# One core, one inference step of a hybrid encoder: four transfers put in other places

## The chip, the core and the metric

The kernel runs on one core of a Trainium2 chip. A core has a matrix engine (PE, TensorE), a vector engine (DVE), a scalar engine (ACT), a general engine (POOL, GpSimd) and a queue engine (SP), which run their own instruction lists in order and wait for one another through semaphores. Transfers are issued from the lists of SP, ACT and POOL and run on the core's 16 DMA engines. The metric is device time in microseconds (us) of the whole program, the median of several runs.

## The reference

```python
h = rmsnorm(x, norm_g)
q, k, v, za, fl, bg, cg, hc, zc = split(h @ w_in)       # columns of one 1024 x 4104 weight
logf = log_sigmoid(fl + b_f);  u = cg * hc
o_a = fox_attention(q, k, v, cumsum(logf))              # 8 heads x 64, causal, with a forget bias
y_c = bg * causal_conv(u, conv_w)                       # depthwise, width 3: conv_w is (3, 512)
x = x + concat(o_a * silu(za), y_c * silu(zc)) @ w_out
y = rmsnorm(x, final_g)
```

This is done for one prompt of 16 meta tokens and 2048 tokens, and for a sample of 8 streams of 16 tokens, each with 256 cached rows. Keys, values, log-forget values and the last convolution inputs are outputs too. All is float32.

## The kernel before

**The work.** Each product of the reference is made of three matmuls: both operands are split into a high and a low part (`hh`, `hl` for tokens, `wh`, `wl` for weights), and high x high, low x high and high x low are summed in a PSUM tile `ps`, of which there are two.

**The stages.** Positions go in two groups. Group 0 has 1280 positions of the prompt and the sample's 128 tokens, group 1 the rest. For each group: `normalise` loads token tiles of 128 rows (`xt`, four buffers), squares them on ACT (`sq`), scales them on DVE and transposes them on PE through `sp`; `values` (first half, `q` = 0) multiplies each of group 0's 11 token tiles with half of the value weights (`wvh`, `wvl`), 24 matmuls a tile; then come keys, queries and gates in slices of 128 columns (`project`), attention units, and the convolution. Projections, attention and the convolution of a group are interleaved on PE. At the end `output` multiplies 17 tiles (the sample's first, then the prompt's 16) with the output weight and normalises the rows.

**What sets the order.** A planner (`Times`) keeps a modelled time for every instruction and every transfer: generators yield a ready time, and `weave` steps the one that is ready soonest. PE's list is the order in which this happens. The lists of DVE, ACT, POOL and SP are sorted by modelled time in `settle`. So a transfer that is moved or that gets cheaper in the model changes the modelled times of what comes after, and with them the order on every engine.

**The parts that the change touches.**
- `load_constants` (L381) loads the mask and, in three transfers (L387), the convolution taps `cw` (channels on partitions: 512 separate 4-byte elements each), and halves them on DVE (L389).
- `split_wv` (L508) splits half of the value weights into `wvh` and `wvl`, and at once stores both to `wv_d` (L535, L536; 1088 and 1024 KB) for group 1, which loads them back. Stores are issued by POOL (`STORES`, L1591).
- `values` (L653): after each tile's matmuls ACT copies `ps` to `sv` (two buffers), which frees `ps`; POOL stores `sv` to the output and the split values `vv` to `v_d`.
- `split_w` (L479) loads the next weight slice `raw` (issued by ACT, L500 to L502), which ACT casts to `wh`; the planner lists this cast on ACT among the copies of `ps` and `sv`.
- `output` (L1364): `load(n)` calls `output_load` (L1337), which loads a tile's concatenated activations `cr` from `cat_d`, casts them to `ch` (ACT) and subtracts to `cl` (POOL). The first tile's are loaded long before (L1353). In `run`, `load_out` (L1577, L1582) loads the rest of the output weight's pieces `o`, three kinds of old weight buffers (`raw`, `wh`, `wl`) serving as room for the first of them, then `fg`, the final norm's weights (L1583), and only then does `output` begin (L1390) and load the second tile's `cr`.

Of the kernel before, what the change touches and what calls it, by code (L numbers as in the profile page):

```python
# [11 lines left out]
F32 = mybir.dt.float32  # L12
F32R = mybir.dt.float32r
BF16 = mybir.dt.bfloat16
AF = mybir.ActivationFunctionType
ALU = mybir.AluOpType
# [4 lines left out]
P = 128  # L21
D = 1024
NC = 8
# [19 lines left out]
OFF_Q, OFF_K, OFF_V, OFF_ZA, OFF_FL = 0, 512, 1024, 1536, 2048  # L43
# [220 lines left out]
def stream(g):  # L264
    return [g, None, False]
# [49 lines left out]
class Step:  # L315
# [7 lines left out]
    def dma(self, out, in_, by=None):  # L323

        if out.dtype == F32R:
            out = out.bitcast(F32)
        if in_.dtype == F32R:
            in_ = in_.bitcast(F32)
        return getattr(self.nc, by or (STORES if out.space == DRAM else "sync")).dma_start(out=out, in_=in_)
# [51 lines left out]
    def load_constants(self, pool):  # L381
        nc, dma = self.nc, self.dma
        mraw = pool.tile([P, P], F32, name="mraw")
        dma(out=mraw, in_=self.cst[:, C_MASK:C_MASK + P])
        nc.vector.tensor_copy(out=self.mask, in_=mraw)
        for i in range(3):
            dma(out=self.cw[:, :, i], in_=self.conv_w[0, i].rearrange("(c p) -> p c", p=P))  # L387

        nc.vector.tensor_scalar(out=self.cw, in0=self.cw, scalar1=0.5, scalar2=None, op0=ALU.mult)  # L389


    def spans(self, ph, c0, n):
# [115 lines left out]
    def split_wv(self, q, raws, pool=None, then=None):  # L508


        nc = self.nc
        wh = self.vp.tile([P, NC, 272], F32R, name="wvh")
        wl = self.vp.tile([P, NC, 256], F32R, name="wvl")
        if OFF_V + 256 * q in self.w_d:
            dh, dl = self.w_d[OFF_V + 256 * q]
            n = 272 if q == 0 else 256
            for k in range(2):
                sl = slice(4 * k, 4 * k + 4)
                self.dma(out=wh[:, sl, :n], in_=dh[:, sl, :n])
                self.dma(out=wl[:, sl], in_=dl[:, sl])  # L520
            return wh, wl
        if q == 0:
            raw8 = pool.tile([P, NC, H], F32, name="raw8")
            self.dma(out=raw8, in_=self.w_v[:, :, OFF_FL:OFF_FL + H])
        for k in range(2):
            raw, sl = raws(k), slice(k * P, k * P + P)
            nc.scalar.copy(out=wh[:, :, sl], in_=raw)
            getattr(nc, V_E).tensor_tensor(out=wl[:, :, sl], in0=raw, in1=wh[:, :, sl].bitcast(F32), op=ALU.subtract)
            if then:
                then()  # L530
        if q == 0:
            nc.vector.tensor_copy(out=wh[:, :, 256:264], in_=raw8)
            nc.vector.tensor_tensor(out=wh[:, :, 264:272], in0=raw8, in1=wh[:, :, 256:264].bitcast(F32), op=ALU.subtract)
        self.w_d[OFF_V + 256 * q] = dh, dl = [self.dram.tile([P, NC, n], F32R, name=f"wv_d{q}{n}") for n in (272, 256)]
        self.dma(out=dh[:, :, :272 if q == 0 else 256], in_=wh[:, :, :272 if q == 0 else 256])  # L535
        self.dma(out=dl, in_=wl)  # L536
        return wh, wl

    def first_values(self, ph, ready, w):
# [113 lines left out]
    def values(self, ph, q, w=None):  # L653

        nc, dma = self.nc, self.dma
        wh, wl = w or self.load_w(OFF_V + 256 * q)
        nh, nl = (272, 264) if q == 0 else (256, 256)
        cols = slice(4 * q, 4 * q + 4)
        for i, (s, r, ct, col) in enumerate(self.token_tiles(ph)):
            while (ph, "tile", i) not in self.there:  # L660
                yield lambda: 0.0 if (ph, "tile", i) in self.there else NEVER
            hh, hl = (t[ph, ct][:, :, col:col + r] for t in (self.hh, self.hl))
            at = self.when(wl, hl, slot=(self.acc, "ps"))
            yield lambda: at() if self.filling + self.held < GTN else NEVER
            self.filling += 1
            ps = self.acc.tile([P, 512], F32, name="ps", bufs=PSB)
            for c in range(NC):
                if c:
                    yield self.when()
                nc.tensor.matmul(ps[:r, :nh], hh[:, c], wh[:, c, :nh], start=(c == 0), stop=False)  # L670
                nc.tensor.matmul(ps[:r, :256], hh[:, c], wl[:, c], start=False, stop=False)
                nc.tensor.matmul(ps[:r, :nl], hl[:, c], wh[:, c, :nl], start=False, stop=(c == NC - 1))
            self.filling -= 1
            sv = self.vp.tile([P, 272], F32, name="sv", bufs=2)
            nc.scalar.copy(out=sv[:r, :nh], in_=ps[:r, :nh])
            if q == 0:
                fl = self.fl[:r, i]
                nc.vector.tensor_tensor(out=fl, in0=sv[:r, 256:264], in1=self.bf[:r], op=ALU.add)
                nc.vector.tensor_tensor(out=fl, in0=fl, in1=sv[:r, 264:272], op=ALU.add)

            vv = self.vp.tile([P, 2, 2, 2, DH], F32R, name="vv", bufs=VVB)
            vw = sv[:r, :256].rearrange("t (p h d) -> t p h d", p=2, h=2)
            for h in range(2):
                nc.vector.tensor_copy(out=vv[:r, :, h, h], in_=vw[:, :, h])
                nc.gpsimd.tensor_tensor(out=vv[:r, :, h, 1 - h], in0=vw[:, :, h], in1=vv[:r, :, h, h].bitcast(F32),
                                        op=ALU.subtract)
            if s < NPOS:
                dma(out=self.nv_p[0, 0, s:s + r, cols].rearrange("t h d -> t (h d)"), in_=sv[:r, :256])
                dma(out=self.v_d[q][:r, :, s // P], in_=vv[:r].rearrange("t p h a d -> t (p h) (a d)"))
                continue  # L690
            dma(out=self.nv_s[0, :, :, cols].rearrange("b s h d -> (b s) (h d)"), in_=sv[:, :256])
            dma(out=self.vs_d[:, q], in_=vv.rearrange("t p h a d -> t (p h a d)"))

    def queries(self, ph, p):
        nc = self.nc
# [668 lines left out]
    def output(self, tiles):  # L1364

        ahead, last = [self.first], len(tiles) - 1

        def load(n):
            if n <= last and n == len(ahead) and self.finished(tiles[n]):
                ahead.append(self.output_load(n, tiles[n]))  # L1370
                return True

        def begin(i):
            while not load(i) and i == len(ahead):
                yield lambda: 0.0 if self.finished(tiles[i]) else NEVER
            t = tiles[i]
            x, y = ((self.x_p[t * P:(t + 1) * P], self.y_p[0, t * P:(t + 1) * P]) if t < 16 else
                    (self.x_s, self.y_s.rearrange("b s d -> (b s) d")))
            xt = self.owk.tile([P, D], F32, name="oxt", bufs=2)
            self.dma(out=xt, in_=x)  # L1380
            return xt, y, *ahead[i]

        def tile(i):
            a = yield from begin(i)
            load(i + 1)
            yield from self.output_half(a, 0)
            yield from self.output_half(a, 1, i == last)
            self.output_norm(a, i == last)

        a, b = (yield from begin(0)), (yield from begin(1))  # L1390
        yield from self.output_half(a, 0)
        yield from self.output_half(b, 0)
        yield from self.output_half(a, 1)
        self.output_norm(a)
        load(2)
        yield from self.output_half(b, 1)
        self.output_norm(b)
        for i in range(2, last + 1):
            yield from tile(i)
# [51 lines left out]
    def run(self, ctx):  # L1451
# [127 lines left out]
        out = stream(self.output([16] + list(range(16))))  # L1579
        for s in att:  # L1580
            assert s[1] or s[2]
        self.nc.step(wload2)  # L1582
        self.dma(out=self.fg, in_=self.final_g.partition_broadcast(P))  # L1583
        weave(order(O4, side, att, wload2, out), out)
# [84 lines left out]
```

## Time and profile before

| | |
|---|---|
| median of 3 runs (lowest, highest) | 1616.66 us (1616.21, 1620.18) |
| profiled execution, its own time | 1619.75 us |
| its span | 1618.0 us |
| busy: PE, weight loads of PE | 1510.7 us (93%), 1360.4 us (84%) |
| busy: DVE, ACT, POOL | 816.9, 594.9, 447.3 us |
| DMA | 256.28 MB, mean 158 GB/s |
| granted TensorE clock, mean | 0.977 |

PE is busy for 93% of the span, and the chain of waits that ended last runs through PE for 78% of it. [...]

### The profile page before, as it was taken

The page shows a single profiled execution, that of the slowest core. Times are in us where ns is not written, and L with a number is a line of the kernel's source. Part 1 is how long each engine was busy: PE and PEld are TensorE (multiplying, and loading weights), DVE is VectorE, ACT ScalarE, POOL GpSimd, SP SyncE. Part 2 cuts the span into 40 slices and gives each one's busy share as a digit, 9 for nine tenths or more (in the row PEclk, how much of TensorE's full clock was granted, in tenths as well). Part 3 has the DMA queues.
Part 4 walks back from the last instruction along what each step waited for, and adds up shares of the span by engine and source line. Part 5 has one row for each costly group of instructions (what it writes and reads, how often), then busy time and mean ns, then how long its engine had stood idle before and what let it go on. Part 6 is the DMA issues. An engine that isn't in the chain of part 4 may idle for free.

```text
span 1618.0 us, 24732 instructions
## 1 busy us (share of the span) xinstructions
PE 1510.7 (93%) x8967; PEld 1360.4 (84%) x8967; DVE 816.9 (50%) x2174; ACT 594.9 (37%) x1108; POOL 447.3 (28%) x706
## 2 busy tenths in 40 slices
PE   4599979998899999999999999999999999899996
PEld 4487969997798888887879899999999999778885
DVE  4443645653466656655341466666656666312222
ACT  3323534433354333332211354555444544211121
POOL 3362424531221132221244123221111111223322
PEclk9799999999899999999999999999999999999998
DMA  9859566556666448984624853556452423444442
GB/s 196 182 145 250 159 152 170 154 160 181 141 150 122 96 129 249 267 239 167 180 88 153 275 169 108 176 173 185 134 154 70 148 72 108 156 156 156 134 140 91
DMA packets 142666, 256.28 MB, mean 158 GB/s; under 512 B 21757, under 2 KB 90901, under 8 KB 139473
## 3 DMA queue, kind: packets, MB, share of 16 engines
q1 hardware_dynamic: 80816, 138.92, 28.5%
q0 software_dynamic: 27536, 85.90, 14.6%
q10 hardware_dynamic: 34192, 29.89, 11.9%
q8 instruction: 71, 1.16, 0.3%
q14 instruction: 51, 0.41, 0.1%
HBM read 154.09 MB, written 100.55 MB: 157 GB/s over the span
## 4 chain that ended last, share of the span: by engine, by line
PE 78%; DMA 13%; issue 3%; POOL 1%; DVE 1%; ACT 1%; SPq 1%; POOLq 0%; ACTq 0%; DVEq 0%
PE ps L278 49%; PE sp L278 11%; PE o L278 9%; PE tp L278 7%; DMA raw<-in_w_in_dram 4%; DMA vb<-v_d 3%; DMA qb<-ql_d 2%; PE tr L278 2%; DMA out_dram<-sv 1%; SPq L278 1%; DMA qa<-qh_d 1%; DMA vn<-in_cache_v_dram 1%; DMA cr<-cat_d 1%; DMA g_bc<-in_norm_g_dram 1%; POOL wvl L278 0%
## 5 line engine op out<-in xcount | busy, mean ns | idle before, releaser
L278 PE MATMUL ps<-hh,wh 128*128 128x512 f32 (+2 forms) x1120 | 423.3, 378 | 0.0
L278 PE MATMUL ps<-hl,wh 128*128 128x512 f32 (+2 forms) x1120 | 407.8, 364 | 0.0
L278 PE MATMUL ps<-hh,wl 128*128 128x512 f32 (+2 forms) x1120 | 407.7, 364 | 0.0
L278 DVE TENSOR_TENSOR pl<-tp,ph 128x512 fp32r<-128x512 f32 (+2 forms) x360 | 198.7, 565 | 137.1 <-ACT ph L278 132.4
L278 DVE TENSOR_SCALAR_CACHE_REDUCE s<-sp 128x384 f32<-128x384 f32 (+3 forms) x360 | 211.3, 600 | 55.1 <-PE sp L278 53.0
L278 ACT CAST ph<-tp 128x512 fp32r<-128x512 f32 (+2 forms) x360 | 169.8, 488 | 181.6 <-PE tp L278 166.7
L278 PEld LDWEIGHTS ps<-hh,wh 128*128 128x128 f32 x1120 | 213.0, 190 | 24.7 <-issue 2.6
L278 PEld LDWEIGHTS ps<-hh,wl 128*128 128x128 f32 x1120 | 212.1, 189 | 20.8
L278 PEld LDWEIGHTS ps<-hl,wh 128*128 128x128 f32 x1120 | 213.1, 190 | 16.7
L278 ACT ACTIVATE s<-s,nm 128x128 f32<-128x128 f32 (+16 forms) x136 | 170.5, 1254 | 132.8 <-DVE nm L278 130.6
L278 PE MATMUL o<-ph,vb 128*128 128x256 f32 (+4 forms) x584 | 165.3, 304 | 15.1 <-DMA vb<-v_d 13.3
L278 PE MATMUL tp<-ident,s 128*128 128x128 f32 (+1 forms) x1224 | 169.5, 263 | 0.0
L278 PE MATMUL sp<-kb,qb 68*128 68x384 f32 (+3 forms) x360 | 141.9, 394 | 17.7 <-DMA qb<-ql_d 8.5
L278 PEld LDWEIGHTS tp<-ident,s 128*128 128x128 f32 (+1 forms) x1224 | 144.4, 141 | 8.6 <-DVE pl L278 0.8
L278 PE MATMUL o<-pl,vb 128*128 128x256 f32 (+4 forms) x584 | 149.5, 284 | 0.3 <-DVE pl L278 0.3
L278 POOL TENSOR_TENSOR gz<-gz,otmp 64x256 f32<-64x256 f32 (+1 forms) x64 | 47.2, 738 | 355.9 <-DVE otmp L278 349.9
L278 PE MATMUL sp<-ka,qa 128*128 128x384 f32 (+3 forms) x360 | 132.2, 367 | 0.0
L278 PEld LDWEIGHTS o<-ph,vb 128*128 128x128 f32 (+1 forms) x584 | 111.6, 191 | 21.8 <-DMA vb<-v_d 15.2
L278 PE MATMUL ps<-o,ch 128*128 128x512 f32 x374 | 118.5, 398 | 8.0 <-ACT ch L278 8.0
L278 PEld LDWEIGHTS o<-pl,vb 128*128 128x128 f32 (+1 forms) x584 | 111.9, 192 | 3.6 <-DVE pl L278 0.5
L278 PE MATMUL ps<-wvh,hh 128*128 128x272 f32 (+3 forms) x288 | 87.0, 302 | 16.6 <-ACT sv L278 16.6
L278 PEld LDWEIGHTS ps<-o,ch 128*128 128x128 f32 x374 | 71.5, 191 | 24.5 <-ACT ch L278 8.5
(221 smaller groups left out, 2154.1 us busy)
## 6 DMA issues: line engine op xcount, KB each, us to landing
raw<-in_w_in_dram ACTq DMA_DIRECT2D x29, 512.0 KB
w_d<-wh ACTq DMA_DIRECT2D x28, 512.0 KB
w_d<-wl POOLq DMA_DIRECT2D x28, 512.0 KB, 9.4
wh<-w_d SPq DMA_DIRECT2D x28, 512.0 KB
wl<-w_d SPq DMA_DIRECT2D x28, 512.0 KB
cr<-cat_d SPq DMA_DIRECT2D x17, 512.0 KB
v_d<-vv POOLq DMA_DIRECT2D x32, 256.0 KB, 3.1
vb<-v_d SPq DMA_DIRECT2D x8, 1024.0 KB
```

The lines of the kernel that those rows point to most:

```text
L278: r = f(*a, **k)
```

## The change

Four edits. (1) The taps are loaded as 12 rows of 128 elements (`taps`), turned by one PE transpose in a side job, and halved on the way out of PSUM. (2) `split_wv` no longer stores the halves of the value weights; `values` does at its end, for group 0. (3) In `output`, `load(1)` stands ahead of everything. (4) In `run`, `output` is stepped once before the remaining output weights are loaded, so that the second tile's `cr` and the two residual tiles `oxt` are issued ahead of them in program order; `fg` still comes after them.

```diff
-        for i in range(3):
-            dma(out=self.cw[:, :, i], in_=self.conv_w[0, i].rearrange("(c p) -> p c", p=P))
-
-        nc.vector.tensor_scalar(out=self.cw, in0=self.cw, scalar1=0.5, scalar2=None, op0=ALU.mult)
+        taps = pool.tile([12, P], F32, name="taps")
+        dma(out=taps, in_=self.conv_w[0].rearrange("i (c p) -> (i c) p", p=P))
+        self.later(self.turn_taps(taps), 0)
+
+    def turn_taps(self, taps):
+        nc = self.nc
+        yield self.when(taps, slot=(self.trp, "tr"))
+        tp = self.trp.tile([P, 4, P], F32, name="tr")
+        nc.tensor.transpose(out=tp[:, 0, :12], in_=taps, identity=self.ident[:12, :12])
+
+        nc.vector.tensor_scalar(out=self.cw, in0=tp[:, 0, :12].rearrange("p (i c) -> p c i", i=3), scalar1=0.5, scalar2=None,
+                                op0=ALU.mult)
...
-        self.w_d[OFF_V + 256 * q] = dh, dl = [self.dram.tile([P, NC, n], F32R, name=f"wv_d{q}{n}") for n in (272, 256)]
-        self.dma(out=dh[:, :, :272 if q == 0 else 256], in_=wh[:, :, :272 if q == 0 else 256])
-        self.dma(out=dl, in_=wl)
         return wh, wl
...
             dma(out=self.vs_d[:, q], in_=vv.rearrange("t p h a d -> t (p h a d)"))
+        if ph == 0:
+
+            self.w_d[OFF_V + 256 * q] = dh, dl = [self.dram.tile([P, NC, n], F32R, name=f"wv_d{q}{n}") for n in (272, 256)]
+            dma(out=dh[:, :, :nh], in_=wh[:, :, :nh])
+            dma(out=dl, in_=wl)
...
+        load(1)
         a, b = (yield from begin(0)), (yield from begin(1))
+        self.loaded = True
         yield from self.output_half(a, 0)
...
             assert s[1] or s[2]
+        self.loaded = False
+        self.nc.step(out)
+        assert self.loaded
         self.nc.step(wload2)
         self.dma(out=self.fg, in_=self.final_g.partition_broadcast(P))
```

What this does to the lists of instructions is seen at three places. The first is POOL's list in the first stage. Before, where `wv_d` is the DRAM room of the value weights, `w_d` that of a weight slice, `ss` a token tile's norm:

```order
L278 TENSOR_TENSOR wvl<-raw,wvh 128x8x128
L278 TENSOR_TENSOR ss<-ss,mhalf 128x1
L278 DMA wv_d_195<-wvl 128x2048
L278 DMA wv_d_194<-wvh 128x2176
L278 TENSOR_TENSOR vv<-sv,vv 128x2x64 x2
L278 DMA w_d_210<-wl 128x1024
L278 DMA out_dram<-sv 128x256
```

In the changed kernel the same two stores stand 29 rows further down POOL's list, each directly ahead of a store that a later token tile waits for:

```order
L278 DMA out_dram<-sv 128x256
L278 DMA v_d_108<-vv 512x1x128
L278 TENSOR_TENSOR vv<-sv,vv 128x2x64 x2
L278 DMA wv_d_891<-wvh 128x2176
L278 DMA out_dram<-sv 128x256
L278 DMA wv_d_892<-wvl 128x2048
L278 DMA v_d_108<-vv 512x1x128
L278 TENSOR_TENSOR vv<-sv,vv 128x2x64 x2
L278 DMA out_dram<-sv 128x256
```

They left the stretch in which the first weight slices and token tiles are loaded, for the second half of the token tiles.

The second place is SP's list of the first stage, as the difference of the two kernels (`xt` are token tiles, `cw` and `taps` the taps):

```order
-L278 DMA xt<-in_x_prompt_dram 128x1024 x5
+L278 DMA xt<-in_x_prompt_dram 128x1024 x3
 L278 DMA mraw<-in_cst_dram 128x128
-L278 DMA cw<-in_conv_w_dram 128x4x1
-L278 DMA xt<-in_x_prompt_dram 128x1024
+L278 DMA taps<-in_conv_w_dram 12x128
+L278 DMA xt<-in_x_prompt_dram 128x1024 x3
 L278 DMA xt<-in_x_sample_dram 128x1024
-L278 DMA cw<-in_conv_w_dram 128x4x1 x2
```

One transfer of 12 rows stands in place of three of 512 elements.

The third is SP's list where the last convolution ends and the output begins. Before (`wh<-w_d` is the last convolution weight, `wh<-o_d`, `wl<-o_d` and `o<-o_d` are pieces of the output weight):

```order
L278 DMA wh<-w_d_8597 128x1024
L278 DMA wl<-w_d_8597 128x1024
L278 DMA wh<-o_d 128x512 x2
L278 DMA wl<-o_d 128x512 x2
L278 DMA wh<-o_d 128x512 x2
L278 DMA wl<-o_d 128x512 x2
L278 DMA fg<-in_final_g_dram 128x1024
L278 DMA oxt<-in_x_sample_dram 128x1024
L278 DMA cr<-cat_d 128x8x128
L278 DMA oxt<-in_x_prompt_dram 128x1024
```

And in the changed kernel:

```order
L278 DMA wh<-w_d_8598 128x1024
L278 DMA wl<-w_d_8598 128x1024
L278 DMA wh<-o_d 128x512 x2
L278 DMA wl<-o_d 128x512 x2
L278 DMA cr<-cat_d 128x8x128
L278 DMA oxt<-in_x_sample_dram 128x1024
L278 DMA wh<-o_d 128x512 x2
L278 DMA oxt<-in_x_prompt_dram 128x1024
L278 DMA wl<-o_d 128x512 x2
L278 DMA fg<-in_final_g_dram 128x1024
```

`cr` moved ahead of the second pair of `wh` and `wl` loads, of `fg` and of the first residual tile.

Beyond these places, PE's list differs from its start through group 0's attention and agrees for its last 5,093 of 8,966 instructions.

## Rows read from the trace of the kernel before

**Rows 1.** The page: busy time, share of the span and instructions of each engine.
```profile
PE 1510.7 (93%) x8967; PEld 1360.4 (84%) x8967; DVE 816.9 (50%) x2174; ACT 594.9 (37%) x1108; POOL 447.3 (28%) x706
```
**Rows 2.** Windows of PE: stretch, length, busy (instructions), granted clock, DMA share, GB/s.
```profile
27.50:110.00 82.50, 60.91 (x403) 0.90 0.70 181
110.00:720.00 610.00, 578.94 (x3412) 0.97 0.65 174
1400.00:1440.00 40.00, 29.24 (x116) 0.87 0.57 194
1440.00:1605.00 165.00, 165.00 (x717) 1.00 0.42 141
```
**Rows 3.** PE's instructions in time, with [idle before <-releaser]: the long stalls.
```profile
55.47 0.59 PE L278 MATMUL ps<-wvh,hh 128*128 128x272 f32 x1 [10.90 <-ACT sv L278]
75.38 1.97 PE L278 MATMUL sp<-ident,xt 128*128 128x128 f32 x8 [5.59 <-DVE hl L278]
1416.45 1.22 PE L278 MATMUL ps<-o,ch 128*128 128x512 f32 x2 [8.05 <-ACT ch L278]
1418.89 0.80 PE L278 MATMUL ps<-o,cl 128*128 128x512 f32 x1 [1.21 <-POOL cl L278]
```
**Rows 4.** Windows of PE, as rows 2: the pace before and after two of those stalls.
```profile
31.50:35.00 3.50, 3.50 (x31) 1.00 1.00 356
55.50:59.00 3.50, 3.50 (x18) 0.58 0.87 164
...
1416.50:1424.00 7.50, 6.29 (x15) 0.52 1.04 363
```
**Rows 5.** ACT's instructions in time, with [idle before <-releaser].
```profile
53.52 1.04 ACT L278 CAST wh<-raw 128x1024 fp32r<-128x1024 f32 x1 [9.38 <-DMA raw<-in_w_in_dram]
...
72.61 0.39 ACT L278 COPY sv<-ps 128x272 f32<-128x272 f32 x1 [2.30 <-DMA out_dram<-sv]
```
**Rows 6.** Chain that ended last, in time: start, length, what (a DMA: issue to landing).
```profile
35.74 17.75 DMA raw<-in_w_in_dram
...
58.24 13.98 DMA out_dram<-sv
...
227.15 10.01 DMA raw<-in_w_in_dram
```
**Rows 7.** DMA issues: queue, count, size of each, median us to landing.
```profile
w_d<-wl POOLq DMA_DIRECT2D x28, 512.0 KB, 9.4
...
out_dram<-sv POOLq DMA_DIRECT2D x34, 128.0 KB, 2.2
...
wv_d<-wvh POOLq DMA_DIRECT2D x1, 1088.0 KB, 20.0
```
**Rows 8.** Windows of 10 us, all engines (PE, PEld, DVE, ACT, POOL), clock, DMA share, GB/s.
```profile
30.00:40.00 10.00, 8.61 (x66) 8.40 (x66) 3.45 (x11) 3.36 (x6) 2.92 (x6) 1.00 0.97 348
...
60.00:70.00 10.00, 9.02 (x52) 7.06 (x50) 7.09 (x11) 5.21 (x9) 3.70 (x6) 1.00 1.02 90
...
90.00:100.00 10.00, 9.51 (x75) 9.36 (x76) 3.98 (x16) 2.33 (x5) 6.46 (x12) 1.00 0.33 108
```
**Rows 9.** SP's DMA issues in time, where the output begins: start, length of issue.
```profile
1392.88 0.86 SPq L278 DMA_DIRECT2D wl<-o_d  x2
1402.70 0.80 SPq L278 DMA_DIRECT2D wh<-o_d  x2
...
1405.50 0.57 SPq L278 DMA_DIRECT2D cr<-cat_d  x1
...
1407.58 12.09 SPq L278 DMA_DIRECT2D o<-o_d  x12
```
**Rows 10.** Who PE waited for from 110 to 720 us: total, times, longest.
```profile
PE o L278 <- DMA vb<-v_d: 13.3, 4, 7.1
PE sp L278 <- DMA qa<-qh_d: 7.3, 1, 7.3
PE sp L278 <- DMA qb<-ql_d: 5.6, 1, 5.6
```

## Prediction

> **What bounds the kernel now.** I read the page first: PE is busy for 93% of the span, and its weight loads for 84% [rows 1]. So only two things can change the time by much: stretches where PE has nothing to do, and stretches where it runs at the lower clock. The windows say where these are [rows 2]. From 27.5 us, when the first value matmuls start, to 110 us PE is idle for 82.5 - 60.9 = 21.6 us; from 110 to 720 us for 31.1 us; in the 40 us in which the output begins for 10.8 us. The list of PE in time says which stalls these are [rows 3]: one of 10.90 us that ends at 55.47, one of 5.59 us that ends at 75.38, one of 8.05 us that ends at 1416.45, with 1.21 us behind it.
>
> Each long stall is followed by half speed. At full clock PE does 31 value matmuls in 3.5 us; after the first stall it does 18 in 3.5 us, at a granted 0.58 [rows 4]. 18 matmuls are worth 2.0 us, so the slow start costs 1.5 us more. [...] At full clock 717 take 165 us [rows 2], 0.23 us each, so 15 are worth 3.5 us; 1.2 us was the second wait, and 2.8 us went to the clock.
>
> Then I asked what each stall waits for. The first: ACT does not copy `sv`, which would free `ps`, because the cast of the next weight slice stands ahead of it on ACT and waits for `raw` until 53.5 us [rows 5]. That transfer took 17.75 us from its issue at 35.74; the same transfer took 10.01 us at 227 [rows 6]. The engines were saturated meanwhile (share 0.97 at 348 GB/s) [rows 8], and the two stores of the value weights, one of which needed 20.0 us to land [rows 7], ran among it. The second: ACT waits with the next `sv` copy until the store of an older `sv` has landed [rows 5]. That store took 13.98 us [rows 6], its kind has a median of 2.2 us [rows 7], and the engines were full from 60 to 70 us (share 1.02) while only 90 GB/s moved [rows 8]: that is what 4-byte elements would do. The third: PE waits for `ch` and `cl` of the second output tile, whose `cr` was issued at 1405.50, behind loads that waited until 1402.70 for the last convolution matmuls to release their room [rows 9].
>
> **The change, part by part.**
>
> Stores moved out of 23 to 45 us. 1088 + 1024 KB at the 348 GB/s of the saturated stretch [rows 8] are 6.1 us of full engines, all of it in the time that `raw` is awaited. Bounds for how much earlier `raw` lands: 0 (it shares with other transfers anyway) and 17.75 - 10.01 = 7.7 us [rows 6]. I take 6. PE's list now also has eight more transposes ahead of the blocked place, worth 1.1 us, and the stall that is left is too short to be followed by half speed as in rows 4: another 1.5 us. Sum -8.6 us, bounds 0 and -12.4 (the stall and its slow start whole). On ACT a token tile's square (about 1 us) now stands ahead of the first `sv` copy, and PE reaches the block later by it; the weight slice comes later still, so it costs nothing as long as the slice is what PE waits for there. If that cover goes, it is 1 us.
>
> Taps by rows. 1,536 elements become 12 rows. What goes is the long landing of the `sv` store and the stall behind it: 5.59 us [rows 3] and 1.6 us of slow start, as after the first stall. Bounds 0 and -7.2; I take the whole, since 13.98 us against a median of 2.2 leaves no other work of that size in the stretch. The transpose and the DVE operation that are new take well under 1 us and stand beside waits; SP issues two transfers fewer.
>
> Stores moved in. They stand on POOL's queue between `sv` stores of later tiles. `sv` has two buffers, so a copy waits for the store of two tiles before. A tile takes 24 matmuls, 2.7 us by rows 4, so a store has some 4.5 us after its issue before it stops ACT. The engines are at 0.33 and 108 GB/s from 90 to 100 us [rows 8]; with 200 GB/s to spare 1088 KB need 5.4 us, and the `sv` store behind them lands about 2.2 us later. That is 7.6 us against 4.5: +2.5 us taken, rounded down for the part already issued. Bounds: 0 (the projections that the new order puts between hide it) and 20.0 us of landing [rows 7] less 4.5, so +15.5.
>
> [...]
>
> Second output tile. `cr` moves behind the loads of 1392.88 [rows 9], with no wait for PE left ahead of it, so it is issued some 11 us earlier, at about 1394. From its issue to the first matmul that had `cl` were 1418.89 - 1405.50 = 13.4 us [rows 3, 9], so `cl` is there at about 1407.4, and PE needs it from 1416.45 - 8.05 = 1408.40. What goes is 8.05 + 1.21 + 2.8 = 12.1 us. What is late next: the second-half pieces of the output weight. Their 12 loads were issued from 1407.58 to 1419.67 [rows 9] and PE now needs the last one at 1408.4 + 24 x 0.23 + 21 x 0.23 = 1418.8. They gain about 1.4 us (512 KB at 363 GB/s, rows 4) by `cr` being gone, and need some 2 us to land: 1.5 us late. So -10.6 us, bounds -7 and -12.1. `fg` and the sample's residual rows are needed only after that; they cost nothing.
>
> Group 0's attention. From 110 to 720 us PE's list is another. It holds the same matmuls. Before, 26 us of waits were for loads of values and queries: six waits, the longest 7.3 us [rows 10]. A wait of this kind with its slow start is 7.3 + 1.5 = 8.8 us. The new list of SP puts a gate load, which waits for POOL, between the two halves of a query load in three places, where before it did in none. I take +2 us for this, bounds one long wait less and two more (-9, +18). The other half's value-weight stores, moved by a few rows in this stretch, lie in these bounds.
>
> Sum: -8.6 - 7.2 + 2.5 - 10.6 + 2 = -21.9 us. Against the profiled execution's own 1619.75 us this is 1597.9. The median of the runs is 3.1 us below that execution, so for a median I take 1616.66 - 21.9 = **1594.8 us**.
>
> **The rivals.**
> *The start's stall comes back* (0.15). The `sv` stores behind `wv_d` land as late as `wv_d` did. For it: those 20.0 us [rows 7], and that they stand right behind `wv_d` on the same queue. Against: the free engines late in this stage [rows 8]. It adds 13 us to the 2.5: 1607.8. [...]
> *The end gains little* (0.08). `cr` is early, but PE waits for the second-half pieces instead, or an unseen wait holds `cr` back, so that the change doesn't do what it says there: 10.6 us lost, 1605.4.
> *Attention gains too* (0.08). One long wait of rows 10 less, and not the 2 us: 1584.0.
> *Slower* (0.06). SP's list runs in order. If the gate loads hold the query loads back, PE stalls at each head change in group 0. At 8.8 us each, two and a half such waits beyond the 2 us eat the gain; with four it is 1594.8 + 35.2 - 2 = 1628. For it: all waits of rows 10 are of this kind. Against: they come to 26 us in all before, over eight heads.
>
> **How the numbers follow.** The forecast with its own bounds has 0.63. My range of 1582 to 1608 takes in the first three rivals and leaves out the slower one and the tails of the bounds, about 2 in 10. A measurement of this kernel can tell about 0.3%, 4.8 us, from no change. Faster by more than that: 0.62 of the forecast, 0.13 + 0.07 + 0.08 of the first three, together 0.90. Within it: 0.05, the tails of these and the slower rival with two or three waits. Slower: 0.05.
>
> **What would show it.** Right: the `raw` transfer issued near 36 us lands in 10 to 13 us; no `sv` store takes over 8 us; the value stage ends some 13 us earlier; PE goes from the first output tile to the second without a wait of over 2 us, and the clock stays at 1.00 there; the attention of group 0 has 22 to 40 us of idle. Wrong: an ACT wait for `out_dram<-sv` of over 5 us behind `wv_d`; `cr` issued only after 1402.70 less the shift; PE waits for query loads that add up to over 25 us between the value stage and group 1.

## The result, and the profile after

The changed kernel took 1601.22 us in the median of four runs (1596.37 to 1604.41), the kernel before 1616.43 us beside it; the ratio is 0.9882, 95% interval 0.9847 to 0.9916. The forecast was 1594.8 us with a range of 1582 to 1608: the sign and the range held, and the gain was smaller than forecast. The profiled execution of the changed kernel is the lowest of its four (mean granted clock 0.984 of full speed) and that of before lies 3 us above its median (0.977), so the two traces lie 23 us apart where the medians lie 15 apart.

The page's first row, and the windows of PE, of the changed kernel (columns as in [rows 2]):

```profile
PE 1509.9 (95%) x8968; PEld 1356.1 (85%) x8968; DVE 814.5 (51%) x2174; ACT 593.7 (37%) x1108; POOL 446.7 (28%) x706
```
```profile
27.50:110.00 82.50, 72.63 (x450) 0.94 0.77 194
110.00:720.00 610.00, 580.34 (x3429) 0.98 0.67 176
1400.00:1440.00 40.00, 37.60 (x154) 1.00 0.57 197
```

PE has the same work as before but for the taps' one transpose. Against [rows 2] it is busy 11.7 us longer up to 110 us, and 8.4 us longer in the 40 us in which the output begins, at a clock of 1.00 in place of 0.87; from 110 to 720 us it is idle for 29.7 us, before 31.1. So the gain sits where it was looked for. The chain of the changed kernel, then ACT and PE in time, against [rows 3, 5, 6]:

```profile
35.78 11.02 DMA raw<-in_w_in_dram
51.55 14.97 DMA out_dram<-sv
81.81 4.41 DMA out_dram<-sv
```
```profile
46.82 1.05 ACT L278 CAST wh<-raw 128x1024 fp32r<-128x1024 f32 x1 [4.36 <-DMA raw<-in_w_in_dram]
...
66.61 0.39 ACT L278 COPY sv<-ps 128x272 f32<-128x272 f32 x1 [6.91 <-DMA out_dram<-sv]
...
82.38 0.39 ACT L278 COPY sv<-ps 128x272 f32<-128x272 f32 x1 [2.39 <-DMA out_dram<-sv]
86.31 0.39 ACT L278 COPY sv<-ps 128x272 f32<-128x272 f32 x1 [3.55 <-DMA out_dram<-sv]
```
```profile
67.05 0.39 PE L278 MATMUL ps<-wvh,hh 128*128 128x272 f32 x1 [3.15 <-ACT sv L278]
```

The second weight slice lands 6.7 us sooner, and the stall of 10.90 us is gone. Half speed is not: it comes earlier, behind two waits of 1.91 and 1.51 us, and in 5 us PE does 24 matmuls where before, at a granted 1.00, it did 31 in 3.9 us of busy time (window of PE in the changed kernel):

```profile
40.00:45.00 5.00, 5.00 (x24) 0.50 1.00 176
```

But the `sv` store that was to be cured by the taps is as slow as ever, 14.97 us against 13.98. ACT waits longer for it than before, 6.91 us, and PE less, 3.15 us in place of 5.59, because projection work now stands ahead of that place in PE's list. This is where the study began.

At the end, SP's issues and PE's instructions:

```profile
1379.91 0.57 SPq L278 DMA_DIRECT2D cr<-cat_d  x1
...
1391.99 10.82 SPq L278 DMA_DIRECT2D o<-o_d  x12
```
```profile
1401.84 0.50 PE L278 MATMUL ps<-o,ch 128*128 128x512 f32 x1
1402.52 0.50 PE L278 MATMUL ps<-o,ch 128*128 128x512 f32 x1 [0.17 <-DMA o<-o_d]
1402.86 0.40 PE L278 MATMUL ps<-o,cl 128*128 128x512 f32 x1
1403.19 0.50 PE L278 MATMUL ps<-o,ch 128*128 128x512 f32 x1
```

`cr` is issued ahead even of the loads that wait for room, and PE no longer waits for `ch`. It waits for the second-half pieces `o` instead, a little at a time: three matmuls take 1.35 us (1401.84 to 1403.19) where at full pace they take 0.70.

And who PE waited for from 110 to 720 us, against [rows 10]: the waits for values went, those for queries came. The last line is from the second trace of the same kernel (after_again, below).

```profile
PE sp L278 <- DMA qb<-ql_d: 16.3, 5, 6.3
PE sp L278 <- issue: 5.0, 1, 5.0
...
PE o L278 <- DMA vb<-v_d: 2.0, 2, 1.5
```
```profile
PE sp L278 <- DMA qb<-ql_d: 25.8, 6, 6.1
```

### The profile page after: what moved, and what is told of

The parts are those of the page before. It is cut to its first block, busy times and chain, and to the rows that moved or that the text cites. A ratio compares the mean times of both kernels' runs of the same rounds, so it can differ in the third digit from the quotient of the medians.

```text
span 1594.6 us, 24718 instructions
## 1 busy us (share of the span) xinstructions
PE 1509.9 (95%) x8968; PEld 1356.1 (85%) x8968; DVE 814.5 (51%) x2174; ACT 593.7 (37%) x1108; POOL 446.7 (28%) x706
## 4 chain that ended last, share of the span: by engine, by line
PE 75%; DMA 13%; issue 5%; SPq 2%; POOL 2%; DVE 2%; ACT 1%; ACTq 0%; POOLq 0%; DVEq 0%
PE ps L278 47%; PE sp L278 11%; PE o L278 9%; PE tp L278 7%; DMA raw<-in_w_in_dram 3%; DMA qb<-ql_d 2%; SPq L278 2%; DMA vb<-v_d 2%; PE tr L278 1%; DMA out_dram<-sv 1%; DMA o<-o_d 1%; DMA kn<-in_cache_k_dram 1%; DMA vn<-in_cache_v_dram 1%; DMA g_bc<-in_norm_g_dram 1%; DMA out_dram<-st 0%
## 5 line engine op out<-in xcount | busy, mean ns | idle before, releaser
L278 PEld LDWEIGHTS tp<-ident,s 128*128 128x128 f32 (+1 forms) x1224 | 144.5, 141 | 11.3 <-ACT s L278 2.3
L278 PEld LDWEIGHTS sp<-kb,qb 68*128 68x128 f32 (+1 forms) x360 | 65.4, 182 | 27.9 <-issue 25.4
```

Of the source, the lines that this page charges most:

```text
L278: r = f(*a, **k)
```

## The experiments

Twelve runs: the change once more, and eleven other kernels. Two devices keep them clean. Some are built so that the planner sees the same transfers as in the kernel they start from, which keeps the order of instructions; a helper, `dma_as(planned out, planned in, issued out, issued in, engine)`, does that, and its `shift` moves an issue within its engine's list by so many modelled ns. And beside the median, which moves by several us with the granted clock (23 runs of the kernel before went from 1617.1 us at 0.977 to 1629.6 us at 0.971), the table has the times at which the profiled execution reaches three places: ACT's last `sv` copy of the first half of the values, its last cast of a weight slice, its last cast of `ch`. Each ratio is to runs of the kernel before that were taken beside it; the row "before" is the first set of these.

| kernel | median us | ratio to before, 95% | last `sv` | last slice | last `ch` | clock |
|---|---|---|---|---|---|---|
| before | 1622.5 | 1 | 99.4 | 837.7 | 1585.9 | 0.977 |
| the change (first set) | 1601.22 | 0.9882 (0.9847, 0.9916) | 93.9 | 824.1 | 1562.5 | 0.984 |
| after_again | 1604.61 | 0.9890 (0.9859, 0.9920) | 94.7 | 830.3 | 1570.3 | 0.980 |
| c_output | 1612.14 | 0.9923 (0.9895, 0.9952) | 100.2 | 837.7 | 1576.8 | 0.979 |
| t_taps | 1624.66 | 1.0004 (0.9980, 1.0028) | 100.8 | 847.1 | 1597.7 | 0.973 |
| s_stores | 1623.39 | 1.0006 (0.9981, 1.0030) | 97.7 | 832.0 | 1582.0 | 0.978 |
| e2_stores | 1611.05 | 0.9933 (0.9910, 0.9956) | 95.8 | 829.7 | 1577.2 | 0.978 |
| z_rows | 1596.42 | 0.9837 (0.9811, 0.9863) | 88.0 | 823.4 | 1561.8 | 0.986 |
| w_late | 1602.89 | 0.9881 (0.9849, 0.9913) | 96.3 | 828.0 | 1569.0 | 0.981 |
| v_sv3 | 1612.61 | 0.9930 (0.9907, 0.9953) | 99.2 | 841.6 | 1580.6 | 0.979 |
| za_swap | 1611.45 | 0.9928 (0.9890, 0.9966) | 97.7 | 833.1 | 1571.7 | 0.980 |
| za_next | 1607.96 (one run) | | 89.1 | 833.9 | 1573.9 | 0.978 |
| za_spread | 1600.35 | 0.9861 (0.9834, 0.9888) | 89.4 | 826.6 | 1566.4 | 0.982 |
| za_late | 1599.89 | 0.9861 (0.9831, 0.9890) | 87.7 | 836.9 | 1578.4 | 0.976 |

### The change again

> The changed kernel once more, as it is. Its four runs so far lay from 1596.4 to 1604.4 us, with the profiled one lowest, at a mean granted clock of 0.984, and the highest at 0.978. If the spread is the clock's, the new runs order themselves by granted clock again, over the same 8 us, and the median of all is near 1601 (ratio 0.988 to 0.992). If the profiled run was one of a kind, the new runs gather above 1600.

The spread goes with the clock: 1601.6 us came at 0.984, 1611.8 and 1609.8 us at 0.979 and 0.978. Between the two traces of this kernel the way to the last slice differs by 6.2 us, and the value stage by 0.8. A difference of a few us after 110 us in one trace is therefore no evidence.

### The output edits alone

```diff
+        load(1)
         a, b = (yield from begin(0)), (yield from begin(1))
+        self.loaded = True
...
+        self.loaded = False
+        self.nc.step(out)
+        assert self.loaded
         self.nc.step(wload2)
```

> The kernel before with edits 3 and 4 alone (the second output tile loaded first); the order of work ahead of the output is that of before. My prediction's term: -10.6 us (bounds -7 and -12.1). By the trace of the change PE gained 8.4 us of busy time from 1400 to 1440 us, so I expect -8 to -11 us, and the start and the middle as before. If the gain at the end was in truth carried over from the start (a rival reading: the output starts earlier, but its weights do not), it is under 4 us.

It reaches the last slice when the kernel before does, at 837.7 us, and the last `ch` 9.1 us sooner. The window and PE's instructions show the gain and what is short of it:

```profile
1400.00:1440.00 40.00, 37.60 (x158) 1.00 0.66 224
```
```profile
1416.69 1.02 PE L278 MATMUL ps<-o,ch 128*128 128x512 f32 x2
1417.54 0.39 PE L278 MATMUL ps<-o,cl 128*128 128x512 f32 x1
...
1423.26 0.62 PE L278 MATMUL ps<-wh,ch 128*128 128x512 f32 x2
```

From 1416.69 to 1423.26 PE does 15 matmuls in 6.6 us that at 0.23 us each (717 in 165 us, [rows 2]) are worth 3.5: the late `o` pieces cost 3.1 us, where the forecast had 1.5.

### The taps alone, in the old order

```diff
-            dma(out=self.cw[:, :, i], in_=self.conv_w[0, i].rearrange("(c p) -> p c", p=P))
+            flat = self.conv_w[0].rearrange("i c -> (i c)").rearrange("(p k) -> p k", k=12)
+            n = 1 if i else P
+            self.dma_as(self.cw[:, :, i], self.conv_w[0, i].rearrange("(c p) -> p c", p=P),
+                        self.cw[:n].rearrange("p c i -> p (c i)"), flat[:n], "sync")
```

> The kernel before, in its own order on every engine, but the three loads of 512 separate elements are replaced by one of 128 pieces of 48 bytes and two of one piece (the tap values land in other places, so the convolution's output is that of other taps). Theory of my prediction: the small elements fill the engines from 60 to 70 us; then the sv store that took 13.98 us lands in under 5 us, the stall of 5.59 us goes, and the time falls by 5 to 7 us. Rival A (the store queues behind a 512 KB weight store in the rings) and rival B (the engines are full with the next weight slice, which is loaded in pieces of 512 bytes): the store still takes 10 to 15 us, the stall of 4 to 6 us stays, and the time moves by 0 to -2 us.

The chain and PE's stall of this kernel:

```profile
58.20 14.81 DMA out_dram<-sv
```
```profile
76.17 1.97 PE L278 MATMUL sp<-ident,xt 128*128 128x128 f32 x8 [5.62 <-DVE hl L278]
```

Nothing moved: the store takes 14.81 us against 13.98, the stall is 5.62 us against 5.59, and the time is the same within 0.3%. The theory of the prediction falls.

### The stores alone, in the old order

```diff
-        self.dma(out=dh[:, :, :272 if q == 0 else 256], in_=wh[:, :, :272 if q == 0 else 256])
-        self.dma(out=dl, in_=wl)
+        n = 272 if q == 0 else 256
+        for o, i in ((dh[:, :, :n], wh[:, :, :n]), (dl, wl)):
+            self.dma_as(o, i, o, i, STORES, issued=False)
         return wh, wl
...
+        if ph == 0:
+            dh, dl = self.w_d[OFF_V + 256 * q]
+            for o, i in ((dh[:, :, :nh], wh[:, :, :nh]), (dl, wl)):
+                self.dma_as(o, i, o, i, STORES, shift=-22000.0, noted=False)
```

> The kernel before, in its own order on PE, DVE, ACT and SP; only POOL's two stores of each half of the value weights are issued near the end of the half's token tiles. Theory of my prediction: the second weight slice lands some 6 us earlier (11 to 12 us from its issue in place of 17.75), the stall of 10.90 us shrinks by as much and its slow start goes: -6 to -9 us. Rival: the slice shares with other loads anyway (or the re-planned order, not the stores, made it land early): it still takes 15 us or more, and the time moves by less than 3 us. In either case the stall of 5.59 us near 75 us stays, or moves with the rest.

The chain, then PE in time:

```profile
35.95 9.03 DMA raw<-in_w_in_dram
49.71 15.97 DMA out_dram<-sv
```
```profile
47.18 0.39 PE L278 MATMUL ps<-wvh,hh 128*128 128x272 f32 x1 [2.26 <-ACT sv L278]
...
68.85 1.97 PE L278 MATMUL sp<-ident,xt 128*128 128x128 f32 x8 [7.12 <-DVE hl L278]
```

The slice lands 8.5 us sooner and the first stall shrinks from 10.90 to 2.26 us, as the theory said. Even this short stall is followed by low clock, as the window of PE behind it shows:

```profile
47.00:50.00 3.00, 2.82 (x14) 0.61 1.04 301
```

PE reaches the next stall as much sooner, and that one ends with a store that is no faster: 7.12 us in place of 5.59. ACT is 8.5 us ahead of before at its fourth `sv` copy, 6.5 at the fifth, 5.4 at the sixth, and, the two stores (issued at 73 and 74 us) now standing between `sv` stores, 1.7 at the last. So of the 8.5 us some 3.1 went at the second stall and 3.7 in the tiles behind the moved stores. The 1.7 us that the trace has left are less than the runs can tell: over 12 runs the time lies between -0.2% and +0.3%. The mechanism was right and the gain was not there.

### The stores alone, planned anew

The diff is edit 2 of the change alone. PE's first 410 instructions are then those of the changed kernel without the taps' transpose.

> The kernel before with edit 2 alone, planned anew: PE's list in the value stage is then that of the changed kernel but for the taps' transpose, and the taps are still loaded in three transfers of 512 elements each. Theory now: the start's gain comes from the stores that moved and from the order that the planner makes of it (projection work ahead of the wait for the sv store), not from the taps. Then the sv store still takes 13 to 16 us, the value stage's last sv copy comes 4 to 6 us earlier than before (99.4 us), about as in the changed kernel, and the time falls by 4 to 14 us. Theory of my prediction (the taps fill the engines): the stall of 5 us or more ahead of 76 us is there again and the value stage ends no earlier than before.

```profile
51.85 15.73 DMA out_dram<-sv
```
```profile
68.43 0.59 PE L278 MATMUL ps<-wvh,hh 128*128 128x272 f32 x1 [4.67 <-ACT sv L278]
```

The store still takes 15.73 us, and the time falls by 0.7%. The same two stores moved in the old order gave nothing, and the intervals do not overlap: the difference is what the planner makes of them, projection work ahead of the second stall and another order in group 0's attention (which of the two gave how much was not tried apart). Together with the output edits alone this is 0.9933 x 0.9923 = 0.986, already as much as the whole change gives; no gain is left that would be the taps'.

### What makes the store late: the slice's pieces, or the queue

Two kernels in the changed kernel's order. In the first the third weight slice comes as whole rows; in the second POOL's 512 KB store ahead of the `sv` store is moved away.

```diff
+        if n0 == OFF_ZA:
+            self.dma_as(raw, self.w_v[:, :, n0:n0 + P], raw.rearrange("p c n -> p (c n)"), self.w_in[0, :P, :NC * P], queue)
...
```

> The changed kernel in its own order, but the third weight slice is loaded as 128 rows of 4096 bytes in place of pieces of 512 bytes (other weights, so what is computed from that slice, part of the gates, is wrong). Rival B (the engines are full with the slice's 512-byte pieces, some 12 us of them): the sv store that took 14.97 us lands within 8 us, ACT's wait of 6.91 us for it and PE's stall of 3.15 us go, and the time falls by 2 to 5 us. [...]

```diff
+            if n0 == OFF_Q:
+                self.dma_as(self.w_d[n0][1], wl, self.w_d[n0][1], wl, STORES, shift=30000.0)
...
```

> The changed kernel in its own order, but the 512 KB store of the second slice's low part, which POOL issued just ahead of the late sv store, is issued some 26 rows later on POOL's queue. [...] Rival B (full engines because of the third slice's pieces): the store lands at most 3 us earlier and the time stays within 3 us.

ACT's first wait for an `sv` store after 50 us, in the first kernel and in the second:

```profile
76.48 0.39 ACT L278 COPY sv<-ps 128x272 f32<-128x272 f32 x1 [2.36 <-DMA out_dram<-sv]
```
```profile
66.87 0.39 ACT L278 COPY sv<-ps 128x272 f32<-128x272 f32 x1 [6.53 <-DMA out_dram<-sv]
```

With rows the long wait is gone (only the two later ones behind `wv_d` are left), the value stage ends 5.9 us sooner than in the changed kernel's first trace, and the median is 8 us below the repeat's (the intervals of the two ratios just meet). Without the weight store ahead, the `sv` store issued at 52.04 us held ACT until 66.87, 14.8 us: the store ahead on its own queue was not the cause. The row that tells this stood in the trace of before all along, in the view of the DMA queues from 57 to 67 us (packets, MB, share of 16 engines; q10 is ACT's queue, the taps go by SP's, q1):

```profile
q10 hardware_dynamic: 833, 0.43, 99.8%
```

and in the changed kernel from 52 to 62 us:

```profile
q10 hardware_dynamic: 775, 0.40, 94.7%
```

ACT's queue alone fills the engines, with 512-byte pieces of 0.947 x 16 x 10 us / 775 = 195 ns each, at 40 GB/s. The view of before has no row for SP's queue, so no piece of the taps moved in those 10 us, and none for POOL's, so the `sv` store that had been issued at 58.24 had not moved a byte by 67 us.

### Those columns, or that moment

```diff
-        getattr(self.nc, queue).dma_start(out=raw, in_=self.w_v[:, :, n0:n0 + P])
+        m0 = {OFF_ZA: OFF_Q, OFF_Q: OFF_ZA}.get(n0, n0)
+        self.dma_as(raw, self.w_v[:, :, n0:n0 + P], raw, self.w_v[:, :, m0:m0 + P], queue)
```

> The changed kernel in its own order, but the second and the third weight slice are loaded from one another's columns (so queries and gates are computed with each other's first weights). Theory 1, the slow pieces belong to those columns of the weight: the load issued at 35.8 us now has pieces of about 180 ns in the mean and lands some 4 us or more later, the one issued at 49.2 us has pieces of about 80 ns, and the sv store issued at 51.5 us lands within 10 us in place of 14.97. Theory 2, the pieces are slow because of what runs beside them at that time: the third load stays at 150 ns or more a piece and the store at 13 us or more.

The second kernel exchanges `OFF_ZA` and `OFF_ZA + P` in the same way.

> The changed kernel in its own order, but the third weight slice and the next slice of the same group (the gates of the next head pair) are loaded from one another's columns, which stand side by side in the weight (so these two pairs of gates are computed with each other's weights). Theory 1, the pieces are slow where those 512 bytes of a row lie: the third load now has pieces of about 80 ns and the sv store lands within 10 us; the later load, some 100 us on, has pieces of about 180 ns. Theory 2, the first load out of that stretch of the rows is slow, whichever of its slices it takes: the third load stays at about 180 ns a piece, the sv store at some 15 us, and the later load stays at 80 to 100 ns.

First za_swap: its chain, and its queue from 41 to 49 us; then za_next from 143 to 151 us, and the changed kernel from 147 to 153 us, where the same load takes its own columns.

```profile
35.93 17.87 DMA raw<-in_w_in_dram
```
```profile
q10 hardware_dynamic: 569, 0.29, 90.4%
```
```profile
q10 hardware_dynamic: 656, 0.34, 101.8%
```
```profile
q10 hardware_dynamic: 964, 0.49, 79.4%
```

Swapped with the second slice, those columns are slow there (203 ns a piece, 17.87 us in place of 11.02, and PE stalls for 6.42 us behind it), and the third load no longer holds the `sv` store. Exchanged with their neighbours, they are slow 91 us later (198 ns a piece, against 79 ns for the neighbours in the changed kernel), and the value stage ends at 89.1 us. Theory 1 of both holds: the slowness goes with the columns.

### Three `sv` buffers

```diff
-            sv = self.vp.tile([P, 272], F32, name="sv", bufs=2)
+            sv = self.vp.tile([P, 272], F32, name="sv", bufs=3)
```

> The changed kernel with three sv buffers in place of two, planned anew. If ACT's waits for sv stores (6.91, 2.39 and 3.55 us) are what is left to gain in the value stage, those waits go and the time falls by 2 to 6 us. If the projections listed between already cover them, it stays within 3 us, or moves by what another order of group 0's attention is worth, up to 8 us either way.

```profile
67.75 0.39 ACT L278 COPY sv<-ps 128x272 f32<-128x272 f32 x1 [7.72 <-DMA out_dram<-sv]
```
```profile
68.19 0.60 PE L278 MATMUL ps<-wvh,hh 128*128 128x272 f32 x1 [4.91 <-ACT sv L278]
```

The wait stayed, one tile later: the planner, which counts a free buffer, lists value tiles ahead and `wv_d` at 54.82 us, a time at which the engines of the changed kernel are full (share 1.02 from 52 to 62 us). By the medians the kernel is some 8 us slower than the repeat of the change; the intervals of the ratios overlap (0.9907 to 0.9953, and 0.9859 to 0.9920), so this is likely and not shown.

### The slow slice in small portions

```diff
+        if n0 == OFF_ZA:
+            self.nc.note(queue, "dma_start", (), dict(out=raw, in_=self.w_v[:, :, n0:n0 + P]))
+            todo = self.nc.order.setdefault(queue, [])
+            for c in range(NC):
+                r = getattr(self.tc.nc, queue).dma_start(out=raw[:, c], in_=self.w_v[:, c, n0:n0 + P])
+                todo.append((self.nc.key + 4500.0 * c, len(todo), r.ins))
...
```

> The changed kernel in its own order, but the third weight slice is loaded in eight transfers of 64 KB that ACT issues among its other work over some 40 us. If the 11 us of engines that this slice takes at once are what makes the sv store late, that store lands within 6 us, ACT's wait of 6.91 us and PE's of 3.15 us shrink to under 2 us each, the value stage ends 3 to 6 us earlier and the time falls by 2 to 6 us against the changed kernel (1601 to 1605 in this study), to a ratio of 0.984 to 0.987. If the eight issues on ACT or a late slice cost as much, it stays at 0.988 to 0.990.

The second kernel also gives the two `wv_d` stores a `shift` of 30000.

> The same as the kernel with the slice in eight transfers, and in addition POOL issues the two stores of the first half's value weights behind the last sv store of that half. The changed kernel's ACT waits of 2.39 and 3.55 us for sv stores behind those two stores go, PE gains 2 to 4 us more in the value stage (last sv copy near 84 to 87 us in place of 93.9), and the time is 0.982 to 0.986 of the kernel before. Against: the 2 MB then run beside the loads for the attention, and the gain is given back there (0.986 or more).

ACT's waits for `sv` stores after 50 us in za_spread:

```profile
77.24 0.39 ACT L278 COPY sv<-ps 128x272 f32<-128x272 f32 x1 [2.80 <-DMA out_dram<-sv]
...
81.81 0.39 ACT L278 COPY sv<-ps 128x272 f32<-128x272 f32 x1 [4.19 <-DMA out_dram<-sv]
```

The wait of 6.91 us is gone, here with the right weights, and the value stage ends 4.5 us sooner; in za_late these two waits go as well and it ends 1.7 us sooner again. Both come to 0.9861. Against the change's 0.9882 and 0.9890 that is 3 to 5 us better, but the intervals overlap; that they beat the changed kernel is likely and not shown. The second step's 1.7 us is not seen in the time.

## Why the prediction was right, and where it was wrong

**Stores moved out, -8.6.** Right as a mechanism: the slice lands 6.7 us sooner where 6 were taken, and the stall is gone. Wrong is the step "too short to be followed by half speed", worth 1.5 us in the sum. In the trace of before a wait of 1.39 us, ending at 36.65, is followed by a granted 1.00 (36.26 to 39.80 us); but a stall of 2.26 us is followed by 0.61 (s_stores), and the changed kernel has its half speed from 40 to 45 us instead. What the term also missed is that the second stall stands behind the first. In the old order 3.1 of 8.5 us went there, and 3.7 more behind the stores in their new place; the sum added the terms as if they were independent.

**Taps, -7.2.** The step that failed, in the words of the prediction: "that is what 4-byte elements would do". Full engines at 90 GB/s said only that the pieces were slow, and these were the 512-byte pieces of one weight slice, on another queue. That 4-byte elements would fill the engines was the author's estimate; no run here shows it. t_taps puts the term at 0 (-0.2% to +0.3%). What the change took from the second stall, 5.59 to 3.15 us, came with the new order (4.67 us in e2_stores, where the taps are as before); the store was never cured.

**The store ahead on the queue.** POOL's 512 KB weight store, which stood in front of the `sv` store, was not the cause: w_late issues it later, and the `sv` store issued at 52.04 us still holds ACT until 66.87, 14.8 us. With the slow slice in rows (z_rows) ACT does not wait for that store. In the trace of before no packet of the store's queue moved from 57 to 67 us, while ACT's queue took 99.8% of the engines.

**Stores moved in, +2.5.** About the right size: behind them the lead in s_stores fell from 5.4 to 1.7 us, which is 3.7, and za_late, without them in between, ends the stage 1.7 us sooner than za_spread.

**Second output tile, -10.6.** The mechanism was right: in c_output `cr` is early and the stall is gone. The 2.8 us of low clock in the sum are what is left of the 7.5 us that 15 matmuls take behind that stall at a granted 0.52 [rows 4], less 3.5 us of work at full pace and 1.2 us of the second wait; in the changed kernel the clock is 1.00 from 1400 to 1440 us. By its trace the term is 9.1 us, and the part that was mis-sized is the late second-half pieces, 1.5 us in the sum and 3.1 measured. By the medians it is 12.5 us (0.9923, so 8 to 17 us), which does not tell 9.1 from 10.6.

**Group 0's attention, +2.** The idle time from 110 to 720 us was 31.1 us before, 29.7 and, in the repeat, 32.0 after. The waits for loads in [rows 10], 26.2 us and half of them for values, became 18.3 us, nearly all for queries, in the first trace and 25.8 us, all for queries, in the repeat. That last number is over the 25 us that the prediction named as a sign of being wrong; the idle time of the stretch stayed all the same, so the term is not shown to be off.

**The sum, -21.9.** Measured: -15.2 us by the first medians and -17.9 by the second. The taps' term was empty, and without it the sum would have been -14.7. That the time still lay in the range, in its upper half, is luck in this respect: the range was wide enough to lose a term of this size. The start came near its forecast with that term empty: PE was busy 11.7 us longer by 110 us where the three terms of the start sum to 13.3, and the new order, for whose projection work ahead of the second stall the sum had no term, filled part of that stall. At the last weight slice the lead was 13.6 us in one trace of the change and 7.4 in the other (11.3 by the sum), and the output gave 9.1 of its 10.6. Of the signs that were named, the `raw` landing, the output without a long wait and the attention's idle time held; "no `sv` store over 8 us" and "some 13 us earlier" did not (14.97 us, 5.5 us). The wait behind `wv_d`, the first rival, came as 2.39 and 3.55 us and not at the size of that rival.

## What to carry to other kernels

Where the DMA engines are full and little moves, read which queue's packets fill them, and how large they are, before naming a cause: one row of the queue view in the trace of before (833 packets of 512 bytes on ACT's queue, 99.8%) would have cleared the taps. Two stalls in series are not two terms: part of what is taken from the first goes to the second unless that moves too (3.1 of 8.5 us in s_stores), and a mechanism that is right in the trace can be worth less in the time than the runs can tell (1.0006, 0.9981 to 1.0030, there). A small store whose buffer is awaited should not be issued just behind a load that fills the engines, as here, where it took 14 to 16 us in place of 2.2; issued in portions, such a load cost ACT no long wait here (the 6.91 us are gone in za_spread), though the gain in time is not shown.

## What the runs showed of the hardware

One slice of the weight, 512 bytes from each of 1024 rows that lie 16,416 bytes apart, loads at 190 to 203 ns a piece with the 16 engines full (90% and more), at each of the three times at which it was loaded; its neighbour, the next 512 bytes of the same rows, takes 79 ns, and the load as rows of 4096 bytes in z_rows some 180 ns a packet (135 packets, 0.48 MB, 15.3% of 10 us). The 128 KB store behind it lands in 14 to 16 us (13.98 in before, 15.97 in s_stores) in place of 2.2 in the median [rows 7].

It is not the only such slice. Of the 30 loads of this form in the changed kernel's trace four have packets of 178 to 195 ns in the mean, the other 26 of 32 to 99 ns, and the same four are slow in the trace of before. First the earliest load (SP's queue, 20 to 30 us), then the loads issued at 407.7 us (411 to 418 us) and at 503.3 us (505 to 512 us):

```profile
q1 hardware_dynamic: 717, 0.37, 98.4%
```
```profile
q10 hardware_dynamic: 574, 0.29, 100.2%
```
```profile
q10 hardware_dynamic: 533, 0.27, 96.1%
```

The four begin at bytes 2048, 6144, 10,272 and 14,368 of the row, about 4096 apart; the slices at 8224 and 12,320, halfway between two of them, are not slow.

All these slices have the same pitch, and two neighbours of the same rows differ here, 195 against 79 ns in the changed kernel; so the pitch alone does not tell the slow ones from the others. Why these columns are slow stays open.
